# One transpose of 128 columns for the two heads' compressed probabilities, in a decoder layer on one core

## The chip, the cores and the metric

The kernel runs on one core of one Trainium2 chip. The metric is the device time of one execution in microseconds, the median of several runs. The engines are named as in the profile: PE is TensorE (PEld its weight loads), DVE is VectorE, ACT is ScalarE, POOL is GpSimd, and SP issues most of the transfers.

## The reference

One decoder layer over 1024 tokens of width 1024: a joint projection, four heads of differential attention, eight heads of sparse attention in two groups of four (three branches with a gate each: compressed, selected, window), an output projection, and a SwiGLU network, each of the two residual sums under a layer norm. The change is in the compressed branch. Its keys and values are 63 blocks, and every query has a probability for each:

```python
s_c = jnp.einsum('btghd,bngd->btghn', q, kc) * scale
p_cmp = masked_softmax(s_c, mask_c[None, :, None, None, :])
o_cmp = jnp.einsum('btghn,bngd->btghd', p_cmp.astype(dt), vc)
...
o = gates[..., 0:1] * o_cmp + gates[..., 1:2] * o_sel + gates[..., 2:3] * o_win
```

With 1024 tokens all 16 selected blocks are taken, so the selected branch is full causal attention.

## The kernel before

All products are in float32 quality made of float32r operands: a value is split in a high part (a cast on ACT, L81) and a low part (value less high part, a subtraction on DVE, L83, sometimes on POOL), and a product of two such values is three products that add up in one bank (L116, L117, L118). Where one operand has 64 rows, its high and low part share the 128 rows of the array.

The program has stages: the first projections, attention with the rest of the projections as filler, the output projection and first norm, and the network. The attention of the sparse heads is cut into units (nsa_units): a pair p of heads (four pairs), a block i of 128 queries (eight) and a kind, 0 for selected and compressed together, 1 for the window. That makes 32 units of kind 0. A unit has two halves.

The front: score products into the banks psS (L323, L326; two buffers, so a product waits until DVE has read the second last one), on DVE the bias of the distance and the running minimum (L329 for the 64 columns of the compressed blocks, L332 for the rest), on ACT the exponential (L346), then the reciprocal of the sum (L405, DVE) and the scaling by gate and reciprocal (L411, POOL). The compressed probabilities of both heads lie in one tile pc, 128 queries x 2 heads x 64 blocks.

The back: probabilities have to stand with the keys on the rows, so PE transposes them by products with the identity into the banks psT (three buffers, L365), ACT and DVE write high and low part into a tile pt (three buffers; L81 and L83, for pc L371 and L372), and PE multiplies with the values into the bank psO (one buffer). L418 is the first of these products, that of the compressed branch, and opens the sum; L426 and L428 add the high and low parts of the other blocks. The values of the compressed branch (vcc) stand twice, on rows 0 to 63 and again on 64 to 127, with their own high and low part side by side in the columns; thus one product takes the high part of the probabilities on one half of the rows and the low part on the other.

Fronts run two units ahead of backs (look = 2 in the phases). Between them stand filler products of the projections, drawn by a generator (pump, step) in proportion to the work done. The code sets priorities; in which order the instructions of each engine stand in the end is decided by a scheduler, which goes by these priorities and its own idea of durations. Each engine then works through its list in order.

Of the kernel before, what the change touches and what calls it, by code (L numbers as in the profile page):

```python
# [11 lines left out]
F32 = mybir.dt.float32  # L12
# [5 lines left out]
P = 128  # L18
# [7 lines left out]
NC = NCMP + 1  # L26
# [11 lines left out]
def layer_kernel(ctx: ExitStack, tc: tile.TileContext, xT, x, w_t, w_vg, w_dv, lam_in, subln,  # L38
# [4 lines left out]
    nc = tc.nc  # L43
# [10 lines left out]
    def ps_t():  # L54
        return psum.tile([P, 512], F32, tag="T", name="psT", bufs=3)
# [88 lines left out]
    with ExitStack() as ctx_a:  # L144
# [213 lines left out]
            nc.scalar.copy(pt[:, :w], tp[:, :w])  # L358
            return pt

        def transposed(srcs, rows=P):

            tp = ps_t()
            for n, s in enumerate(srcs):
                nc.tensor.transpose(tp[:rows, n * P:(n + 1) * P], s, ident)  # L365
            w = len(srcs) * P
            pt = pt_tile().rearrange("p (h n) -> p h n", h=2)
            if rows == P:
                split(tp[:, :w], pt[:, 0, :w], pt[:, 1, :w])
            else:  # L370
                nc.scalar.copy(pt[0:rows, 0, :w], tp[0:rows, :w])  # L371
                nc.vector.tensor_sub(pt[rows:2 * rows, 0, :w], tp[0:rows, :w], pt[0:rows, 0, :w].bitcast(F32))  # L372
            return pt

        def nsa_units(p, qt, K, V):
# [7 lines left out]
            def make(i, kind):  # L383
                nb = i + 1 if kind == 0 else min(i + 1, WIN_BLOCKS)
                j0 = i + 1 - nb
                width = nb * P
                ts = []

                def front():
                    dist = dsel[:, 1024 - width:] if kind == 0 else dwin[:, 640 - width:]  # L390
                    m = small([P, 4], "m", 4)
                    r = small([P, 4], "r", 4)
                    ts.extend(t_tiles(width))
                    if kind == 0:
                        pc = pa.tile([P, 2, NC], F32, tag="pc", name="pc", bufs=3)
                        ts.append(pc)
                    for a in range(2):
                        ms, rs = ([t[:, n:n + 1] for n in (a, 2 + a)] for t in (m, r))
                        cmp = (pc[:, a, :], dcmp[:, 56 - 8 * i:56 - 8 * i + NC], ms[1]) if kind == 0 else None
                        scores(q_of(qt, i, a), K[kind], j0 * P, width, dist, sl[a], ms[0], ts[a], cmp)  # L400
                        exps(ts[a], width, ms[0], rs[0])
                        if kind == 0:
                            exps(pc[:, a, :], NC, ms[1], rs[1])
                    nr = 2 if kind else 4
                    nc.vector.reciprocal(r[:, :nr], r[:, :nr])  # L405
                    for a in range(2):
                        for n, t in ((1 + kind, ts[a][:, :width]), (0, pc[:, a, :] if kind == 0 else None)):
                            if t is not None:
                                gc = heads[a] * 3 + n
                                c = a if n else 2 + a  # L410
                                nc.gpsimd.tensor_scalar(t, t, r[:, c:c + 1], gates[:, i, gc:gc + 1],  # L411
                                                        op0=ALU.mult, op1=ALU.mult)

                def back(fill):
                    if kind == 0:
                        state["po"] = po = ps_o()
                        ptc = transposed([ts[2][:, a, :] for a in range(2)], rows=64)
                        nc.tensor.matmul(po[:, :256], lhsT=vcc[g], rhs=ptc[:, 0, :256], start=True, stop=False)  # L418
                    po = state["po"]
                    for jj in range(0, nb, 2):  # L420
                        js = range(jj, min(jj + 2, nb))
                        pt = transposed([ts[a][:, j * P:(j + 1) * P] for j in js for a in range(2)])
                        for n, j in enumerate(js):
                            v = V[kind][:, (j0 + j) * P:(j0 + j + 1) * P]
                            last = kind == 1 and j == nb - 1
                            nc.tensor.matmul(po[:, :256], lhsT=v, rhs=pt[:, 0, n * 256:(n + 1) * 256],  # L426
                                             start=False, stop=False)
                            nc.tensor.matmul(po[:, :256], lhsT=v, rhs=pt[:, 1, n * 256:(n + 1) * 256],  # L428
                                             start=False, stop=last)
                        fill((jj + len(js)) / nb)  # L430
                    if kind == 1:
                        tmp = small([P, 256], "tmp", 3)[0:64, :]
                        nc.scalar.copy(tmp, po[64:128, :256])
                        nc.vector.tensor_add(tmp, po[0:64, :256], tmp)
                        for a in range(2):
                            nc.sync.dma_start(mix_d[i, a * 64:(a + 1) * 64, 4 + p, :], tmp[:, a * P:(a + 1) * P])

                return front, back, 2.0 * nb + 1
# [823 lines left out]
```

## Time and profile before

| | |
|---|---|
| time, median of 3 runs | 1308.02 us (1307.05 to 1309.11) |
| span of the profiled execution | 1306.1 us |
| instructions | 20483 |
| granted TensorE clock, mean | 0.999 |
| transposes of pc (L365) | 64, from 98 to 398 us |
| copies L371, subtractions L372, products L418 | 32 each |
| HBM read, written | 116.18 MB, 57.15 MB |

The median is 1.9 us above the span of the profiled execution; the span runs from the first to the last instruction, and no other time of that execution is known. The page gives busy time by engine, a chain of work that ended last, and groups of instructions by line. A line can be that of a helper: L81 and L83 split values for many callers, told apart by their tiles.

### The profile page before, as it was taken

Reading aid. Unit: us, or ns where it says so; the run is one execution under the profiler, and the core shown is the slowest. Engines: PE = TensorE matmul, PEld = TensorE weight load, DVE = VectorE, ACT = ScalarE, POOL = GpSimd, SP = SyncE. Lnnn points to the kernel's source line nnn. Section 1 sums busy time; section 2 is a strip of 40 time slices with the busy share of each in tenths; the row PEclk is TensorE's granted clock in tenths of the full one; section 3 lists DMA queues with packets and bytes.
Section 4 is the critical chain, followed back from the end, with each engine's and each line's share of the span. In section 5 each row is a group of like instructions: output and inputs, shape, how many; then the busy total and the mean of one; then the engine's idle time right before and its main releaser. Section 6 shows DMA issues by size and latency. Waiting matters only on the chain.

```text
span 1306.1 us, 20483 instructions
## 1 busy us (share of the span) xinstructions
PE 1287.4 (99%) x6955; PEld 1108.2 (85%) x6955; DVE 917.0 (70%) x1956; ACT 652.0 (50%) x1398; POOL 465.3 (36%) x499
## 2 busy tenths in 40 slices
PE   9999999999999999999999999999999999999997
PEld 7897999988988889788887888888888888888886
DVE  5548867778778666674787677776767768555588
ACT  5348867878777556652344333333333335533330
POOL 4514534545345446643623313232231222000071
PEclk9999999999999999999999999999999999999999
DMA  9412011211112135623214566555546549768641
GB/s 356 146 27 49 9 50 54 56 48 48 33 56 70 49 82 148 220 93 107 87 69 144 192 225 234 193 172 172 180 150 205 185 172 344 267 199 290 194 169 65
DMA packets 86842, 183.13 MB, mean 140 GB/s; under 512 B 10577, under 2 KB 19153, under 8 KB 86609
## 3 DMA queue, kind: packets, MB, share of 16 engines
q1 hardware_dynamic: 86736, 181.82, 42.8%
q8 instruction: 55, 0.90, 0.3%
q14 instruction: 51, 0.41, 0.1%
HBM read 116.18 MB, written 57.15 MB: 133 GB/s over the span
## 4 chain that ended last, share of the span: by engine, by line
PE 93%; DVE 4%; ACT 1%; issue 1%; DMA 0%; POOL 0%; DVEq 0%; ACTq 0%; POOLq 0%
PE psM L116 11%; PE psM L118 11%; PE psM L117 10%; PE psT L116 6%; PE psT L117 6%; PE psT L118 6%; PE psS L118 6%; PE psS L117 6%; PE psS L116 6%; PE psT L365 4%; PE psS L323 3%; PE psS L326 3%; PE psO L428 2%; PE psO L426 2%; PE psO L481 2%; PE psO L118 2%
## 5 line engine op out<-in xcount | busy, mean ns | idle before, releaser
L346 ACT ACTIVATE t<-t,m 128x384 f32<-128x384 f32 (+7 forms) x192 | 144.2, 752 | 58.8 <-DVE m L332 53.9
L411 POOL TENSOR_SCALAR t<-t,r,gates 128x640 f32<-128x640 f32 (+7 forms) x128 | 100.2, 789 | 186.9 <-DVE r L405 107.8
L116 PE MATMUL psM<-big,w 128*128 128x512 f32 x304 | 120.6, 397 | 0.3 <-DVE slot L171 0.3
L118 PE MATMUL psM<-big,w 128*128 128x512 f32 x304 | 120.1, 396 | 0.0
L117 PE MATMUL psM<-big,w 128*128 128x512 f32 x304 | 119.9, 394 | 0.0
L323 PE MATMUL psS<-slot,q 128*128 128x320 f32 (+10 forms) x304 | 111.5, 369 | 2.9 <-DVE m L332 2.7
L1010 POOL TENSOR_TENSOR half<-half,half 128x512 f32<-128x512 f32 x22 | 33.3, 1515 | 206.6 <-ACT half L1009 206.6
L83 DVE TENSOR_TENSOR pt<-psT,pt 128x512 fp32r<-128x512 f32 (+1 forms) x152 | 91.4, 615 | 13.6 <-ACT pt L81 12.5
L326 PE MATMUL psS<-slot,q 128*128 128x320 f32 (+10 forms) x304 | 99.2, 329 | 0.0
L81 ACT CAST pt<-psT 128x512 fp32r<-128x512 f32 (+1 forms) x152 | 77.6, 526 | 23.3 <-PE psT L365 10.7
L81 ACT CAST big<-slot 128x1024 fp32r<-128x1024 f32 (+1 forms) x54 | 54.4, 1019 | 65.8 <-DVE slot L1002 51.2
L83 DVE TENSOR_TENSOR op<-op 128x1024 fp32r<-128x1024 f32 x44 | 61.3, 1400 | 36.9 <-ACT op L81 36.4
L83 DVE TENSOR_TENSOR big<-slot,big 128x1024 fp32r<-128x1024 f32 (+1 forms) x54 | 63.5, 1181 | 29.5 <-ACT big L81 29.3
L365 PE MATMUL psT<-ident,t 128*128 128x128 f32 x528 | 82.7, 273 | 1.1 <-DVE pt L83 0.9
L81 ACT CAST op<-op 128x1024 fp32r<-128x1024 f32 x44 | 45.9, 1051 | 63.1 <-DMA op<-t_d 60.5
L332 DVE CUSTOM_DVE_ANT_0 t<-psS,dsel 128x384 f32<-128x384 f32 (+9 forms) x128 | 62.4, 493 | 15.0 <-PE psS L326 9.6
L428 PE MATMUL psO<-pt,slot 128*128 128x256 f32 x264 | 72.2, 295 | 0.1
L1014 POOL TENSOR_TENSOR half<-half,half 128x512 f32<-128x512 f32 x22 | 36.5, 1661 | 98.8 <-DVE half L1013 98.6
L426 PE MATMUL psO<-pt,slot 128*128 128x256 f32 x264 | 71.6, 288 | 0.0
L118 PEld LDWEIGHTS psM<-big,w 128*128 128x128 f32 x304 | 57.1, 188 | 11.5
L81 ACT CAST big<-big 128x1024 fp32r<-128x1024 f32 (+1 forms) x49 | 44.2, 912 | 45.3 <-DMA big<-t_d 37.1
L116 PEld LDWEIGHTS psM<-big,w 128*128 128x128 f32 x304 | 57.3, 188 | 10.9 <-DVE slot L171 0.7
(370 smaller groups left out, 3969.0 us busy)
## 6 DMA issues: line engine op xcount, KB each, us to landing
a_d<-slot SPq DMA_DIRECT2D x77, 256.0 KB, 3.1
t_d<-slot SPq DMA_DIRECT2D x77, 256.0 KB, 2.2
q<-q SPq DMA_DIRECT2D x48, 256.0 KB, 2.9
slot<-in_w_up_dram SPq DMA_DIRECT2D x22, 512.0 KB, 3.8
slot<-in_w_down_dram SPq DMA_DIRECT2D x22, 512.0 KB, 3.9
op<-a_d SPq DMA_DIRECT2D x44, 256.0 KB, 3.4
op<-t_d SPq DMA_DIRECT2D x44, 256.0 KB, 4.1
big<-a_d SPq DMA_DIRECT2D x33, 256.0 KB, 3.2
```

The lines of the kernel that those rows point to most:

```text
L81: nc.scalar.copy(hi, src)
L83: eng.tensor_sub(lo, src, hi.bitcast(F32))
L116: nc.tensor.matmul(acc, lhsT=ah, rhs=bh, start=first, stop=False, skip_group_check=more)
L117: nc.tensor.matmul(acc, lhsT=ah, rhs=bl, start=False, stop=False, skip_group_check=more)
L118: nc.tensor.matmul(acc, lhsT=al, rhs=bh, start=False, stop=last, skip_group_check=more)
L323: mm = nc.tensor.matmul(ps[:, :c + part], lhsT=q[0], rhs=k[:, ks], start=True, stop=False)
L326: nc.tensor.matmul(ps[:, :c + part], lhsT=q[1], rhs=k[:, ks], start=False, stop=True)
L346: nc.scalar.activation(t[:, :width], t[:, :width], AF.Exp, bias=m, scale=-1.0, accum_out=r)
L365: nc.tensor.transpose(tp[:rows, n * P:(n + 1) * P], s, ident)
L411: nc.gpsimd.tensor_scalar(t, t, r[:, c:c + 1], gates[:, i, gc:gc + 1], op0=ALU.mult, op1=ALU.mult)
L426: nc.tensor.matmul(po[:, :256], lhsT=v, rhs=pt[:, 0, n * 256:(n + 1) * 256], start=False, stop=False)
L428: nc.tensor.matmul(po[:, :256], lhsT=v, rhs=pt[:, 1, n * 256:(n + 1) * 256], start=False, stop=last)
```

## The change

The two transposes of pc, one for each head with 64 columns, become one of pc as a matrix of 128 columns. The first head's transposed probabilities then come out on rows 0 to 63 of the bank, the second head's on rows 64 to 127, both in the same 128 columns. The copy and the subtraction, which took both heads at once (64 rows x 256 columns), are now made for each head alone (64 rows x 128 columns), so there are two copies and two subtractions. The high part stays on the head's own rows, the low part goes to the other half; the product that uses pt is the same, as the values stand on both halves.

```diff
-        def transposed(srcs, rows=P):
+        def transposed(srcs):
...
-            if rows == P:
-                split(tp[:, :w], pt[:, 0, :w], pt[:, 1, :w])
-            else:
-                nc.scalar.copy(pt[0:rows, 0, :w], tp[0:rows, :w])
-                nc.vector.tensor_sub(pt[rows:2 * rows, 0, :w], tp[0:rows, :w], pt[0:rows, 0, :w].bitcast(F32))
+            split(tp[:, :w], pt[:, 0, :w], pt[:, 1, :w])
+            return pt
+
+        def transposed_cmp(pc):
+
+            tp = ps_t()
+            nc.tensor.transpose(tp[:, :P], pc.rearrange("p a n -> p (a n)"), ident)
+            pt = pt_tile()[:, :2 * P]
+            for a in range(2):
+                own, other = slice(a * NC, (a + 1) * NC), slice((1 - a) * NC, (2 - a) * NC)
+                cs = slice(a * P, (a + 1) * P)
+                nc.scalar.copy(pt[own, cs], tp[own, :P])
+                nc.vector.tensor_sub(pt[other, cs], tp[own, :P], pt[own, cs].bitcast(F32))
             return pt
...
-                        ptc = transposed([ts[2][:, a, :] for a in range(2)], rows=64)
-                        nc.tensor.matmul(po[:, :256], lhsT=vcc[g], rhs=ptc[:, 0, :256], start=True, stop=False)
+                        nc.tensor.matmul(po[:, :256], lhsT=vcc[g], rhs=transposed_cmp(ts[2]), start=True, stop=False)
```

The lines move: the transpose of pc is L374 now, the copies are L379, the subtractions L380, the product of the compressed branch L425 (was L418), the value products L433 and L435 (were L426 and L428); L365, L323 to L346, L81 and L83 keep theirs.

The scheduler puts the instructions of every engine in another order from the first transpose of pc on, until about the end of attention; behind that the order is the same. Two places show how.

The first is PE's list at the first unit of kind 0. Numbers tell buffers apart (psS_1046 and psS_1051 are the two score banks, pt_916 is what L418 uses). Before:

```order
L365 MATMUL psT_913<-ident_74,pc_853 64x128
L365 MATMUL psT_920<-ident_74,t_852 128x128 x3
L365 MATMUL psT_913<-ident_74,pc_853 64x128
L365 MATMUL psT_920<-ident_74,t_852 128x128
L365 MATMUL psT_939<-ident_74,t_852 128x128 x2
L323 MATMUL psS_1046<-slot1_237,q_464 128x128
L326 MATMUL psS_1046<-slot1_237,q_464 128x128
L323 MATMUL psS_1051<-slot1_237,q_465 128x128
L326 MATMUL psS_1051<-slot1_237,q_465 128x128
L418 MATMUL psO_912<-pt_916,vcc0_86 128x256
L426 MATMUL psO_912<-pt_925,slot2_549 128x256
L365 MATMUL psT_966<-ident_74,t_875 128x128 x4
```

Behind these rows come the next score products, L323 into psS_1086. The same place in PE's list now:

```order
L374 MATMUL psT_913<-ident_74,pc_853 128x128
L365 MATMUL psT_921<-ident_74,t_852 128x128 x4
L365 MATMUL psT_940<-ident_74,t_852 128x128 x2
L323 MATMUL psS_1048<-slot1_237,q_464 128x128
L326 MATMUL psS_1048<-slot1_237,q_464 128x128
L323 MATMUL psS_1053<-slot1_237,q_465 128x128
L326 MATMUL psS_1053<-slot1_237,q_465 128x128
L323 MATMUL psS_1088<-slot0_236,q_464 128x288
L326 MATMUL psS_1088<-slot0_236,q_464 128x288
L323 MATMUL psS_1094<-slot0_236,q_464 128x288
L326 MATMUL psS_1094<-slot0_236,q_464 128x288
```

The next score products follow at once, with no product between, and L418, now L425, stands further back, behind six more transposes of t and twelve filler products of 512 columns.

The second place is ACT's list at the second unit, with the engines that an instruction waits for in brackets. Before:

```order
L81 CAST pt<-psT 128x256 [waits DVE_49,PE_49]
L346 ACTIVATE pc,r<-pc,m 128x64 [waits DVE_49,Pool_49]
L371 CAST pt<-psT 64x256 [waits PE_49,Activation_49]
L346 ACTIVATE t,r<-t,m 128x512 [waits DVE_49]
L346 ACTIVATE pc,r<-pc,m 128x64 [waits DVE_49]
```

The one copy waits for the transpose. The same unit in ACT's list now:

```order
L81 CAST pt<-psT 128x256 [waits PE_49]
L379 CAST pt<-psT 64x128 [waits PE_49]
L346 ACTIVATE pc,r<-pc,m 128x64 [waits DVE_49]
L379 CAST pt<-psT 64x128 [waits DVE_49]
L346 ACTIVATE t,r<-t,m 128x512 [waits DVE_49]
```

Of the two copies the first waits for the transpose and the second for DVE: the count that it waits for is reached by the subtraction of the same unit's first head. An exponential stands between them.

More of the change, by code (lines that the diff above doesn't have):

```diff
@@ L359, in transposed_whole @@
             return pt
-        def transposed(srcs, rows=P):
+        def transposed(srcs):
             tp = ps_t()
             for n, s in enumerate(srcs):
-                nc.tensor.transpose(tp[:rows, n * P:(n + 1) * P], s, ident)
+                nc.tensor.transpose(tp[:, n * P:(n + 1) * P], s, ident)
             w = len(srcs) * P
             pt = pt_tile().rearrange("p (h n) -> p h n", h=2)
-            if rows == P:
-                split(tp[:, :w], pt[:, 0, :w], pt[:, 1, :w])
-            else:
-                nc.scalar.copy(pt[0:rows, 0, :w], tp[0:rows, :w])
-                nc.vector.tensor_sub(pt[rows:2 * rows, 0, :w], tp[0:rows, :w], pt[0:rows, 0, :w].bitcast(F32))
+            split(tp[:, :w], pt[:, 0, :w], pt[:, 1, :w])
[9 more added lines that the diff above has]
+                nc.vector.tensor_sub(pt[other, cs], tp[own, :P], pt[own, cs].bitcast(F32))
             return pt
```

## Prediction

> **What bounds the kernel now.** The views were read in this order: the page's busy times and chain, a table of busy time by stretch, the timeline of the matrix engine (PE) around the changed products, the groups of instructions by shape, and the waits of PE in the stretch that holds the change. From the page, the head, the busy times and the chain by engine:
>
> ```profile
> span 1306.1 us, 20483 instructions
> PE 1287.4 (99%) x6955; PEld 1108.2 (85%) x6955; DVE 917.0 (70%) x1956; ACT 652.0 (50%) x1398; POOL 465.3 (36%) x499
> PE 93%; DVE 4%; ACT 1%; issue 1%; DMA 0%; POOL 0%; DVEq 0%; ACTq 0%; POOLq 0%
> ```
>
> PE is the bound: the chain that ended last lies on it for 93%. The rest, 5%, is on the vector (DVE) and scalar (ACT) engines. The changed products stand between 98 and 398 us (first and last start in the row of L365 below), so the stretch from 95 to 408 us is the one to read. The table by stretch gives busy time of PE, PEld, DVE, ACT and POOL, the granted clock and the DMA share:
>
> ```profile
> 95.00:408.00 313.00, 308.74 (x2113) 281.61 (x2112) 239.87 (x845) 239.28 (x645) 145.99 (x212) 1.00 0.18 45
> 408.00:600.00 192.00, 188.32 (x1156) 166.01 (x1156) 129.83 (x364) 111.13 (x292) 99.63 (x98) 1.00 0.39 112
> ```
>
> PE shows 4.3 us idle in 313; DVE is busy for 77% and ACT for 76%, more than in the stretch behind. So a product less on PE should be worth its spacing, and DVE and ACT have room, but not much.
>
> **What a product is worth.** Durations of products overlap, so the price is the distance of starts. The timeline of PE, with start, length and instruction:
>
> ```profile
> 247.37 0.28 PE L426 MATMUL psO<-pt,slot 128*128 128x256 f32 x1
> 247.49 0.38 PE L365 MATMUL psT<-ident,t 128*128 128x128 f32 x2
> 247.63 0.36 PE L428 MATMUL psO<-pt,slot 128*128 128x256 f32 x1
> 247.83 0.27 PE L426 MATMUL psO<-pt,slot 128*128 128x256 f32 x1
> 247.94 0.28 PE L428 MATMUL psO<-pt,slot 128*128 128x256 f32 x1
> 248.06 0.38 PE L365 MATMUL psT<-ident,pc 128*64 128x128 f32 x2
> 248.20 0.45 PE L323 MATMUL psS<-slot,q 128*128 128x448 f32 x1
> 248.48 0.36 PE L326 MATMUL psS<-slot,q 128*128 128x448 f32 x1
> 248.69 0.28 PE L426 MATMUL psO<-pt,slot 128*128 128x256 f32 x1
> 248.80 0.36 PE L323 MATMUL psS<-slot,q 128*128 128x448 f32 x1
> 249.00 0.37 PE L326 MATMUL psS<-slot,q 128*128 128x448 f32 x1
> ```
>
> A 256-wide product takes 0.12 us to the next start (247.83 to 247.94, 247.94 to 248.06) and a 448-wide one 0.20 (248.80 to 249.00). Two transposes of t with the product behind them take 247.83 - 247.49 = 0.34, so 0.22 without it; two of pc take 248.48 - 248.06 = 0.42, less 0.20, again 0.22. A transpose costs 0.11 us, with 64 columns as with 128.
>
> Its weight load, from the groups of line L365 (least, median and longest ns; first and last start):
>
> ```profile
> L365 PEld LDWEIGHTS psT<-ident,t x528: 137/140/147, 98.6 to 404.9; 128*128 128x128 f32 x176
> L365 PEld LDWEIGHTS psT<-ident,pc x64: 108/110/113, 98.4 to 397.6; 128*64 128x64 f32 x64
> ```
>
> The load of 128 columns takes 30 ns more, but two of t take no longer than two of pc, so the work of PE hides it; were it in the open, 32 of them would cost 1.0 us.
>
> **Term 1, the products: 32 fewer at 0.11 us, -3.5 us.** All are on PE, in a stretch where PE sets the pace.
>
> **The copies and subtractions.** The groups by shape (count, busy us, mean ns, idle before them and what ended it): the old forms, then the nearest rows for 64 x 128, and last a pair of groups that alternate as the new ones will.
>
> ```profile
> L371 ACT CAST pt<-psT 64x256 fp32r<-64x256 f32 x32 | 11.5, 361 | 4.2 <-PE psT L365 4.0
> L372 DVE TENSOR_TENSOR pt<-psT,pt 64x256 fp32r<-64x256 f32 x32 | 13.4, 418 | 1.5 <-ACT pt L371 0.7
> L358 ACT COPY pt<-psT 128x128 f32<-128x128 f32 x8 | 2.1, 265 | 0.6 <-PE psO L481 0.5
> L485 DVE COPY od<-psO 128x128 f32<-128x128 f32 x31 | 8.9, 288 | 15.4 <-PE psO L481 15.1
> L83 DVE TENSOR_TENSOR slot<-psT,slot 128x64 fp32r<-128x64 f32 x32 | 6.8, 223 | 11.3 <-ACT slot L81 11.2
> L81 ACT CAST slot<-psT 128x64 fp32r<-128x64 f32 x32 | 6.5, 213 | 11.4 <-PE psT L118 6.1 <-DVE slot L83 5.2
> ```
>
> No 64 x 128 form is in the trace; it lies between 128x64 and 64x256, and 128 columns cost 265 ns on ACT and 288 on DVE. So each unit adds 2 x 265 - 361 = 169 ns on ACT and 2 x 288 - 418 = 158 ns on DVE: 5.4 and 5.1 us in all (ends: with the 128x64 rows 2.1 and 0.9, with the old price twice 11.6 and 13.4). [...]
>
> The second copy also waits. In the order of ACT after the change it stands behind a wait for DVE, that of the unit's first subtraction, so copy, subtraction, copy, subtraction follow one another, four steps in place of two. Queued behind it on ACT are exponentials (L346) and other copies of transposed blocks (L81), for which DVE and then PE wait. The nearest row for it is the last above: there ACT stood 5.2 us for DVE over 32 copies, 0.16 each, so 32 second copies give 5.2 us more idle ACT.
>
> **Term 2, load and waits beside PE: +0.7 us.** That is 15.7 us in all (5.4 + 5.1 + 5.2). DVE and ACT put 5% of 1306, 65 us, on the chain out of 1569 busy, 4.2%; that share of 15.7 is 0.7. The ends are 0 and, if every ACT wait reached PE, 5.2. The cover is the work queued on PE; where it is gone a unit would pay about 0.8 us (a copy of 0.27, a turn of DVE of some 0.5).
>
> **What the new order does to the waits of PE.** The waits of PE and its weight loads in 95 to 408 us (total, times, longest; one wait can be in both views):
>
> ```profile
> PE psS L323 <- DVE m L332: 2.3, 4, 0.9
> PE psO L418 <- DVE pt L372: 0.4, 1, 0.4
> PEld psS L323 <- DVE m L332: 4.1, 9, 1.1
> PEld psO L428 <- DVE pt L83: 2.4, 9, 0.4
> PEld psO L418 <- DVE pt L372: 1.6, 4, 0.6
> ```
>
> I counted the products between a producer and its user in PE's order, at the spacings above. **Term 3, the wait of L418: -0.5 us.** Units with under 2 us of products between the transpose of pc and L418 fall from five to one, and the rows have five waits, 2.0 us; the first is the place that the order shows. But the way to L418 now has four steps. How long turns on two engines take, one unit shows: its pc products are those of 248.06 above.
>
> ```profile
> 249.17 0.37 ACT L371 CAST pt<-psT 64x256 fp32r<-64x256 f32 x1
> 250.97 0.42 DVE L372 TENSOR_TENSOR pt<-psT,pt 64x256 fp32r<-64x256 f32 x1
> 256.30 0.28 PE L418 MATMUL psO<-pt,vcc 128*128 128x256 f32 x1
> ```
>
> The copy began 1.1 us and the subtraction 2.9 us behind the product, and L418 8.2 us behind: here the longer way stays covered by 4.9 us. Ends: all 2.0 us gone, or as much again; I take a quarter of the gain. **Term 4, score products: +1.5 us.** Those that follow the last use of their bank by under 1 us rise from 16 to 22 (the order shows two). Thirteen waits took at most 6.4 us, 0.49 each, so six more cost 0 to 2.9; half is taken, since many are only just under. **Term 5, value products: +0.7 us.** Transposes with under 1.5 us to their first product rise from 7 to 12; at 0.27 a wait (2.4 over 9) 0 to 1.3, half taken. From 408 us on the order changes by places only, up to about 600 us, and not behind that: 0, give or take 1. The edit issues no DMA, and the queues of POOL and SP keep their instructions.
>
> **The sum.** -3.5 + 0.7 - 0.5 + 1.5 + 0.7 = -1.1 us. The profiled span is 1306.1; the median of the three runs, 1308.02 us, holds 1.9 us more around it, which nothing here touches. So 1308.0 - 1.1 = 1306.9 us, a span of 1305.0. The bound for a difference, 0.2%, is 2.6 us; the runs before spread over 2.1.
>
> **The rivals.** *Faster:* terms 2, 4 and 5 are nothing, since the order leaves enough work in front of each user, and L418 waits no more: -3.5 - 2.0 = -5.5, 1302.5 us. For it: PE idles only 4.3 us in the stretch; against: DVE and ACT were already the ones that PE waited for. *Slower:* the second copy blocks ACT until DVE comes to the first subtraction, and L418 and the score products come too early. The price: five units at 0.8 us, 4.0, and the upper ends 2.9 and 1.3, less 3.5: +4.7, 1312.7 us. It decides from 0.11 us of new PE waiting a unit (3.5 / 32) for no gain, and from 0.19 (6.1 / 32) for a loss over 2.6. *The wide product is no cheaper than two:* then term 1 is 0 and the sum +2.4, 1310.4; the equal spacing of pc and t speaks against it. [...]
>
> **How the numbers follow.** The forecast has 0.40 (its own range 1305.4 to 1309.0), faster as above 0.32, slower 0.24, the wide product 0.02, the drain 0.02. Faster by over 0.2% is 0.34, within it 0.42 (the wide product ends there), slower 0.24. The range, 1302.0 to 1312.0 us, takes in the fast rival and most of the slow one, and leaves out the drain and a loss over 4 us.
>
> **What would show it.** Right: L374 32 times, PE's spacing at them 0.11; copies of 64x128 near 265 ns, subtractions near 288; PE's busy time some 3.5 us shorter, with idle and waits for L332 and L83 up by 2 to 3 us. Wrong: waits of L425 (the old L418) over 3 us in total, or ACT standing at L379 for DVE over 8 us (slower); or waits of PE in the stretch no longer than before (faster).

## The result, and the profile after

The kernel after takes 1318.06 us (median of 4 runs, 1316.38 to 1319.8), the kernel before 1307.72 us beside it (1307.05 to 1309.11). The ratio is 1.008, with a 95% interval from 1.0068 to 1.0092: 10.3 us slower, where 1.1 us faster was forecast, and above the stated range, which ended at 1312.0.

From the page of the kernel after, the head, the busy times and the chain by engine:

```profile
span 1314.7 us, 20477 instructions
PE 1289.0 (98%) x6923; PEld 1105.2 (84%) x6923; DVE 923.6 (70%) x1988; ACT 657.1 (50%) x1430; POOL 465.0 (35%) x499
PE 90%; DVE 5%; ACT 2%; issue 2%; DMA 1%; POOL 0%; SPq 0%; DVEq 0%; ACTq 0%; POOLq 0%
```

32 products are gone (6955 to 6923), but PE's busy time has not fallen (1287.4 to 1289.0), where some 3.5 us less was expected, and its part of the chain went from 93% to 90%. The single instructions came out as priced. The groups by shape of the new copies and subtractions (count, busy us, mean ns, idle before them and what ended it):

```profile
L379 ACT CAST pt<-psT 64x128 fp32r<-64x128 f32 x64 | 16.5, 257 | 8.5 <-DVE pt L380 4.0 <-PE psT L374 2.5 <-PE psO L425 1.3
L380 DVE TENSOR_TENSOR pt<-psT,pt 64x128 fp32r<-64x128 f32 x64 | 18.4, 288 | 6.3 <-ACT pt L379 4.4
```

257 and 288 ns a piece, where 265 and 288 were expected, and ACT stands 4.0 us for the subtraction (5.2 expected). The transpose is where it should be too. PE's timeline at one of the 32 (start, length):

```profile
258.75 0.30 PE L326 MATMUL psS<-slot,q 128*128 128x288 f32 x1
258.89 0.27 PE L374 MATMUL psT<-ident,pc 128*128 128x128 f32 x1
258.99 0.39 PE L425 MATMUL psO<-pt,vcc 128*128 128x256 f32 x1
```

0.10 us to the next start. So the prices of single instructions were right, and the time went elsewhere. To find the place I cut the run by two marks that stand in every version: the first transpose of pc, and the first and last transpose of a block of the differential heads (L355). The group of L355 (least, median, longest ns; first and last start), first of before, then of after:

```profile
L355 PE MATMUL psT<-ident,t x144: 270/272/328, 405.5 to 596.0; 128*128 128x128 f32 x144
```

```profile
L355 PE MATMUL psT<-ident,t x144: 270/273/332, 411.0 to 604.6; 128*128 128x128 f32 x144
```

The last one comes 8.6 us later, and the span is longer by 8.6 (1306.1 to 1314.7): all of the loss between these two executions lies in front of 604.6 us. The profiled execution of the kernel after took 1316.38 us at a mean granted clock of 0.999 and the other three 1317.69 to 1319.8 at 0.998 and 0.997, so the traces show 8.6 us of the 10.3 between the medians. The loss is in two stretches. The table by stretch (length, then busy time of PE, PEld, DVE, ACT, POOL, the clock and the DMA share), of before and of after:

```profile
98.60:405.50 306.90, 302.63 (x2075) 276.17 (x2074) 236.26 (x828) 234.69 (x628) 142.17 (x203) 1.00 0.18 46
405.50:596.00 190.50, 186.82 (x1159) 165.21 (x1158) 130.63 (x368) 112.17 (x294) 99.02 (x99) 1.00 0.39 112
```

```profile
98.50:411.00 312.50, 303.84 (x2043) 273.10 (x2042) 241.99 (x860) 240.55 (x660) 141.39 (x203) 1.00 0.18 45
411.00:604.60 193.60, 187.38 (x1159) 165.55 (x1158) 130.60 (x368) 111.77 (x294) 99.54 (x99) 1.00 0.37 110
```

In the stretch with the changed units, 5.6 us more (306.9 to 312.5), with 32 products fewer and PE's idle time doubled, from 4.3 to 8.7 us. In the stretch behind it, 3.1 us more (190.5 to 193.6), and there the products are the same 1159: the edit changes no work in it, only the order. The waits of PE and of its weight loads between 95 and 411 us (total, times, longest):

```profile
PE psT L365 <- DVE pt L83: 3.0, 6, 1.3
PE psS L323 <- DVE m L332: 2.3, 4, 0.8
PE psS L323 <- issue: 1.1, 1, 1.1
PE psS L323 <- DVE m L329: 0.3, 1, 0.3
PE psT L365 <- DVE pt L380: 0.3, 1, 0.3
PE psO L425 <- DVE pt L380: 0.2, 1, 0.2
```

```profile
PEld psS L323 <- DVE m L332: 6.1, 15, 0.9
PEld psT L365 <- issue: 3.6, 7, 1.7
PEld psO L435 <- DVE pt L83: 3.3, 12, 0.4
PEld psS L323 <- issue: 2.3, 5, 1.3
```

The same rows of the kernel before, where they were not shown yet (95 to 410 us):

```profile
PE psT L365 <- DVE pt L83: 0.9, 2, 0.7
```

```profile
PEld psT L365 <- issue: 1.3, 5, 0.4
...
PEld psS L323 <- issue: 0.5, 2, 0.3
```

The product that uses the new copies, L425, hardly waits (0.2). The waits that grew belong to other work: the transposes of t, which stand until DVE has freed a bank (0.9 before, 3.0 now), the weight loads of score products (4.1 to 6.1), and weight loads for whose wait the trace names no releaser ("issue", 1.8 to 5.9). That pointed at the order of the lists, not at the changed instructions.

### The profile page after: what moved, and what is told of

It is laid out like the page before. It is cut to its first block, busy times and chain, and to the rows that moved or that the text cites. A ratio compares the mean times of both kernels' runs of the same rounds, so it can differ in the third digit from the quotient of the medians.

```text
span 1314.7 us, 20477 instructions
## 1 busy us (share of the span) xinstructions
PE 1289.0 (98%) x6923; PEld 1105.2 (84%) x6923; DVE 923.6 (70%) x1988; ACT 657.1 (50%) x1430; POOL 465.0 (35%) x499
## 4 chain that ended last, share of the span: by engine, by line
PE 90%; DVE 5%; ACT 2%; issue 2%; DMA 1%; POOL 0%; SPq 0%; DVEq 0%; ACTq 0%; POOLq 0%
PE psM L116 10%; PE psM L118 10%; PE psM L117 10%; PE psT L116 6%; PE psT L117 6%; PE psT L118 6%; PE psS L118 6%; PE psS L116 6%; PE psS L117 6%; PE psT L365 4%; PE psS L323 3%; PE psS L326 3%; PE psO L435 2%; PE psO L433 2%; PE psO L116 2%; PE psO L118 2%
## 5 line engine op out<-in xcount | busy, mean ns | idle before, releaser
L346 ACT ACTIVATE t<-t,m 128x384 f32<-128x384 f32 (+7 forms) x192 | 144.0, 751 | 55.0 <-DVE m L332 51.3
L323 PE MATMUL psS<-slot,q 128*128 128x320 f32 (+10 forms) x304 | 111.4, 370 | 7.8 <-DVE m L332 4.0
L83 DVE TENSOR_TENSOR pt<-psT,pt 128x512 fp32r<-128x512 f32 (+1 forms) x152 | 91.7, 614 | 11.3 <-ACT pt L81 10.5
L83 DVE TENSOR_TENSOR op<-op 128x1024 fp32r<-128x1024 f32 x44 | 60.6, 1386 | 41.4 <-ACT op L81 41.1
L81 ACT CAST pt<-psT 128x512 fp32r<-128x512 f32 (+1 forms) x152 | 77.5, 527 | 24.1 <-PE psT L365 13.5
L81 ACT CAST big<-slot 128x1024 fp32r<-128x1024 f32 (+1 forms) x54 | 54.4, 1018 | 68.4 <-DVE slot L1009 54.8
L365 PE MATMUL psT<-ident,t 128*128 128x128 f32 x528 | 81.8, 273 | 3.6 <-DVE pt L83 3.0
L83 DVE TENSOR_TENSOR big<-slot,big 128x1024 fp32r<-128x1024 f32 (+1 forms) x54 | 63.8, 1188 | 28.4 <-ACT big L81 28.4
L81 ACT CAST op<-op 128x1024 fp32r<-128x1024 f32 x44 | 45.9, 1051 | 66.7 <-DMA op<-t_d 61.2
L323 PEld LDWEIGHTS psS<-slot,q 128*128 128x128 f32 x304 | 57.4, 189 | 17.0 <-DVE m L332 9.0
L435 PE MATMUL psO<-pt,slot 128*128 128x256 f32 x264 | 71.3, 292 | 0.2
L433 PE MATMUL psO<-pt,slot 128*128 128x256 f32 x264 | 70.8, 287 | 0.0
L365 PEld LDWEIGHTS psT<-ident,t 128*128 128x128 f32 x528 | 61.6, 140 | 9.2 <-issue 3.6
L116 PEld LDWEIGHTS psM<-big,w 128*128 128x128 f32 x304 | 57.2, 188 | 12.4 <-ACT w L81 1.6
```

Source lines behind the costliest of these rows:

```text
L81: nc.scalar.copy(hi, src)
L83: eng.tensor_sub(lo, src, hi.bitcast(F32))
L116: nc.tensor.matmul(acc, lhsT=ah, rhs=bh, start=first, stop=False, skip_group_check=more)
L323: mm = nc.tensor.matmul(ps[:, :c + part], lhsT=q[0], rhs=k[:, ks], start=True, stop=False)
L346: nc.scalar.activation(t[:, :width], t[:, :width], AF.Exp, bias=m, scale=-1.0, accum_out=r)
L365: nc.tensor.transpose(tp[:, n * P:(n + 1) * P], s, ident)
```

## The experiments

The theory at this point (A): the loss belongs to the order that the scheduler made, and the edit's own work gains about what was forecast. Its rival (B): the serial copy, subtraction, copy, subtraction of each unit is the loss. To tell them apart, work and order have to be set apart. A table with each engine's list is put in and kept by chaining every instruction to the one ahead of it in the table:

```diff
+    pin(tc)
...
+    for engine, places in zip(engines, lists):
+        mine = [i for i in traced if i.engine == engine and "PoolBoundary" not in type(i).__name__]
+        for a, b in zip(places, places[1:]):
+            tc.add_manual_dep(mine[b], mine[a].name, how, reason="pinned order")
```

"In the order of" means this below, and "free" that the scheduler decides. All experiments together, each against the kernel before in the same comparison (1307.5 to 1307.8 us). "Wide product alone" leaves out the second head's compressed probabilities, so it is a measure of time only. Two rows whose intervals overlap are not told apart by these runs:

| run | work | order | us | ratio, 95% interval |
|---|---|---|---|---|
| e1 | old | of after | 1318.62 | 1.0086 (1.0072 to 1.0099) |
| e9 | wide product alone | of after | 1316.35 | 1.0071 (1.0059 to 1.0084) |
| e5 | new, copies first | of after | 1345.58 | 1.0286 (1.0272 to 1.0300) |
| e2 | new | of before | 1333.12 | 1.0193 (1.0179 to 1.0207) |
| e3 | new, copies first | of before | 1316.09 | 1.0066 (1.0052 to 1.0079) |
| e8 | as e3, pc scaled early | of before | 1310.19 | 1.0022 (1.0013 to 1.0031) |
| e6 | split alone | of before | 1322.99 | 1.0119 (1.0105 to 1.0132) |
| e7 | split alone, copies first | of before | 1308.79 | 1.0010 (1.0002 to 1.0019) |
| e10 | old | free, another | 1308.07 | 1.0001 (0.9992 to 1.0009) |
| e11 | split alone, copies first | free | 1308.83 | 1.0006 (0.9998 to 1.0015) |
| e15 | split alone | free | 1324.70 | 1.0130 (1.0116 to 1.0143) |
| e14 | wide product alone | free | 1311.47 | 1.0031 (1.0019 to 1.0042) |
| e4 | new, copies first | free | 1315.07 | 1.0057 (1.0044 to 1.0069) |
| e12 | new, pc scaled first | free | 1312.30 | 1.0036 (1.0023 to 1.0049) |
| e16 | new, both of these | free | 1312.67 | 1.0039 (1.0025 to 1.0052) |
| e13 | old | of after behind 405 us only | 1313.20 | 1.0039 (1.0026 to 1.0051) |
| e17 | new | of before behind 411 us only | 1316.06 | 1.0063 (1.0049 to 1.0077) |
| e18 | as e16 | of before behind 406 us only | 1314.38 | 1.0048 (1.0035 to 1.0060) |

### The order apart from the work: e1, e9

> The work of the kernel before (64 transposes of 64 columns, 32 copies and 32 subtractions of 64x256), with every engine's list fixed in the order of the kernel after: the two transposes stand where the one of 128 columns stands, the copy where the first copy stands, the subtraction where the second one stands. Theory A, the order: the loss of 10.3 us is the order's, and the edit's own work gains about as much as forecast (3.5 less 0.7), so this takes the loss and pays the products again: 1318 + 3 = about 1321 us (1318 to 1324). Theory B, the work: the serial copy, subtraction, copy, subtraction of each unit delays PE, and the order does nothing: about 1308 us (1306 to 1310). Between, half each: about 1313.

Measured 1318.62, 11.2 us over before. Its groups of L365 and L355:

```profile
L365 PE MATMUL psT<-ident,pc x64: 270/272/276, 97.9 to 402.9; 128*64 128x128 f32 x64
L355 PE MATMUL psT<-ident,t x144: 270/272/328, 411.0 to 606.7; 128*128 128x128 f32 x144
```

All 64 narrow transposes are there, nothing of the edit's work is, and the marks at 411.0 and 606.7 are late as in the kernel after. Rival B falls: the order alone loses as much as the whole change. But of A's 3 us of gain in this order, only 1318.62 - 1318.06 = 0.6 is there, less than the intervals can tell from nothing. The wide product by itself tells more:

```diff
-            for a in range(2):
-                ...
-                nc.scalar.copy(pt[own, cs], tp[own, :P])
-                nc.vector.tensor_sub(pt[other, cs], tp[own, :P], pt[own, cs].bitcast(F32))
+            both = tp[0:NC, None, :P].to_broadcast([NC, 2, P])
+            nc.scalar.copy(hi, both)
+            nc.vector.tensor_sub(lo, both, hi.bitcast(F32))
```

> The wide product alone: one transpose of 128 columns in place of two of 64, but one copy and one subtraction of 64x256 as before, every list in the order of the kernel after (the run of the old work in that order, with two narrow transposes at this place, took 1318.6 us). The copy and the subtraction read the first head's rows twice, so the second head's compressed probabilities are replaced by the first's; nothing else is changed. If a transpose less is worth its spacing of 0.11 us where PE is the bound: 1318.6 - 3.5 = 1315.1 (1314.3 to 1316). If the wide product is no cheaper, or what it frees is lost in waits at once: 1318 to 1319.

1316.35, just above the range that its spacing gave (1314.3 to 1316): 32 transposes fewer are worth 2.3 us here by the medians. In the two traces the stretch from the first transpose of pc to the first L355 is 1.8 us shorter (313.1 in e1, 311.3 in e9). That is half to two thirds of the 3.5. The split with its chain then costs 1318.06 - 1316.35 = 1.7. Neither 2.3 nor 1.7 is clear of the intervals; only the first step of the account, 11.2 for the order, is. The three steps go from the kernel before to the kernel after, so that their sum, 11.2 - 2.3 + 1.7 = 10.6, comes near the 10.3 by construction and proves nothing further.

### The new work in the old order: e2, e3, e8

The transpose takes the place of the second narrow one (in nine units a place nearer to the first). In e3 the copies are written first:

```diff
-            for a in range(2):
-                ...
-                nc.scalar.copy(pt[own, cs], tp[own, :P])
-                nc.vector.tensor_sub(pt[other, cs], tp[own, :P], pt[own, cs].bitcast(F32))
+            for own, other, cs in halves:
+                nc.scalar.copy(pt[own, cs], tp[own, :P])
+            for own, other, cs in halves:
+                nc.vector.tensor_sub(pt[other, cs], tp[own, :P], pt[own, cs].bitcast(F32))
```

> The work of the kernel after (32 transposes of 128 columns, 64 copies and 64 subtractions of 64x128, the second copy still waiting for the first subtraction), with every engine's list fixed in the order of the kernel before: the transpose stands where the second narrow one stood (in nine units a little earlier, next to the first), the two copies where the copy stood, the two subtractions where the subtraction stood. Theory A, the order: 1308 - 3.5 + 0.7 = about 1305 us (1303 to 1308). Theory B, the work: about 1318 us (1315 to 1321).

> As the run before (new work, old order), but both copies are written ahead of both subtractions, so that the second copy no longer waits for DVE. Theory A, the order: the wait is hidden anyway, so the same as with the wait, within 1.5 us: about 1305 us. Theory B, the work in a serial chain: the wait is the cost, so about 1306 where the run with the wait takes 1318.

1333.12 and 1316.09. Theory A as it stood falls here: it wanted 1305 for both. B misses both times as well (1318 and 1306), though it has the sign of the difference. The old order is no home for the new work, and in it the wait that A held to be hidden costs 17.0 us. Part of e3's loss is the place: four transposes stood for GpSimd's scaling of the second head (PE in e3, 95 to 410 us):

```profile
PE psT L374 <- POOL pc L419: 4.6, 4, 1.5
```

> The new work with copies first in the old order, as run once at 1316.1 us; there four transposes of pc stood 4.6 us for GpSimd's scaling of the second head, since they stand where the first narrow transpose stood. Here, in the nine units with such a place, the scaling of pc's second head is moved ahead of the scaling of t's second head, which gives the transpose 0.9 to 1.1 us. If those waits are an effect of the place only, and the gain of the products is real: 1310 to 1313. If the old order cannot take the wide transpose at all: 1315 to 1317.

The edit is one of the table: the scaling of pc's second head moves one place up in GpSimd's list, at eight places (the tables of e3 and e8 differ in eight pairs of neighbours there and nowhere else). 1310.19, as the place alone would have it (1310 to 1313), and the row above is down to 0.3. That is 5.9 us for four waits and what hung on them, and it is the best time that the whole new work reached; still 2.7 over before.

### The copies and subtractions alone: e6, e7, e11, e15

```diff
-                nc.scalar.copy(pt[0:rows, 0, :w], tp[0:rows, :w])
-                nc.vector.tensor_sub(pt[rows:2 * rows, 0, :w], tp[0:rows, :w], pt[0:rows, 0, :w].bitcast(F32))
+                for n in range(2):
+                    cs = slice(n * P, (n + 1) * P)
+                    nc.scalar.copy(pt[0:rows, 0, cs], tp[0:rows, cs])
+                    nc.vector.tensor_sub(pt[rows:2 * rows, 0, cs], tp[0:rows, cs], pt[0:rows, 0, cs].bitcast(F32))
```

The narrow transposes stay. In e7 and e11 the loop over n is made twice, copies first.

> The kernel before in its own order, the two narrow transposes kept, but with the copy and the subtraction of each unit made as two of 64x128, the second copy waiting for the first subtraction; the copies stand next to each other, and so do the subtractions. This is the split alone, without the wide product and without a new order. By the forecast's term for it: 1308.2 (0.7 more). If the chain costs as much as the earlier pair of runs in the old order differed by (1333.1 with the wait, 1316.1 without): 1318 to 1325.

> As the run before (the split alone, old order, narrow transposes), with both copies ahead of both subtractions, so without the second copy's wait. What is left is 5 us more of busy time on ACT and on DVE each. If only the wait costs: 1307.5 to 1308.5. If busy time costs PE by its whole amount: 1312 to 1313.

1322.99 and 1308.79: 14.2 us for the wait, 1.3 (0.3 to 2.5 by its interval) for 32 instructions more on each engine. The forecast's 1308.2 for e6 is out, and the range taken from e2 and e3 holds; e7 is 0.3 above its range for the wait alone. The groups of the copies, first with the wait, then without:

```profile
L373 ACT CAST pt<-psT 64x128 fp32r<-64x128 f32 x64 | 16.4, 257 | 34.1 <-DVE pt L374 30.4 <-PE psT L365 3.5
```

```profile
L373 ACT CAST pt<-psT 64x128 fp32r<-64x128 f32 x64 | 13.2, 256 | 4.2 <-PE psT L365 4.0
```

With the two copies next to each other in ACT's list, the second stands 30.4 us for DVE, 0.95 each, and everything behind it on ACT stands with it. In one unit of e6 the first copy ends at 202.84 us, DVE comes to the subtraction at 203.44, behind a subtraction of 0.69 us for another block (L83), and the second copy starts at 203.76. The same two with the scheduler free:

> Narrow transposes, the copy and the subtraction split in two each, copies first, with the scheduler free. The same work in the order of the kernel before took 1308.8 us, so the difference to that is the new order's alone (1877 of PE's places changed). If orders that the scheduler makes differ by up to 10 us on their own: 1303 to 1319, off from 1308.8 by over 2. If only the order of the kernel after is a bad one by chance of its chain: 1307 to 1311.

> Two narrow products, copy and subtraction split in two each with the second copy waiting for the first subtraction, the scheduler free (2633 of PE's places changed). With copies first, so without that wait, the free order took 1308.8 us. If the chain leads the scheduler to costly orders: 1313 to 1322. If the wide product does: 1308 to 1311.

1308.83 and 1324.70. Without the wait another order (1877 places of PE changed) takes what the old order takes, to 0.04 us. With the wait the free order costs 15.9 us more (1313 to 1322 was expected if the chain leads to costly orders), though ACT's wait is nearly gone from it (e15):

```profile
L373 ACT CAST pt<-psT 64x128 fp32r<-64x128 f32 x64 | 16.3, 255 | 8.0 <-DVE pt L374 3.1 <-PE psT L365 3.0 <-PE psO L420 1.4
```

The scheduler moved the second copy away from the first until it seldom waited; the time did not come back with the wait. The kernel after has the same row with 4.0 us. How far its lists are built around that chain, e5 shows.

> The kernel after in its own order on every engine, but with both copies written ahead of both subtractions, so that the second copy no longer waits for the first subtraction (every copy and subtraction keeps its place in its list). The old work in this order took 1318.6 us and the new work 1318.1. Theory A, the order sets the time and the chain of copy, subtraction, copy, subtraction hides the gain of the products in it: the rest of the 3.5 us comes out, about 1315 to 1316. Theory A2, the order alone, with the chain hidden: 1318, no change. Theory B, the chain is the whole loss: about 1308.

1345.58, a miss for all three. With copies first, it is the first subtraction that waits for the second copy, and in this order the second copy stands some rows further back in ACT's list (in one unit the first copy starts at 252.70, two copies of L81 follow, and the second starts at 253.94). DVE's wait, 95 to 420 us:

```profile
DVE pt L380 <- ACT pt L378: 36.8, 27, 3.7
```

So this run does not price the chain; it shows that an order fits one sequence of the four steps and not the other.

### Other orders and the two parts, free: e10, e4, e12, e14, e16

e10 writes the narrow transposes in the other sequence; e12 scales pc first, and e16 is that with copies first:

```diff
-            for n, s in enumerate(srcs):
+            for n, s in list(enumerate(srcs))[::-1 if rows < P else 1]:
```

```diff
-                        for n, t in ((1 + kind, ts[a][:, :width]), (0, pc[:, a, :] if kind == 0 else None)):
+                        for n, t in ((0, pc[:, a, :] if kind == 0 else None), (1 + kind, ts[a][:, :width])):
```

> The kernel before with the two narrow transposes written in the other sequence, second head first. The work is the same to the last instruction; the scheduler draws another order, with 597 of PE's places changed between the first pc transpose and about 300 us (the change under study alters 2586, up to the end of attention). If a new order by itself moves the time by us: anywhere from 1303 to 1314, off from 1307.5 by over 1.5. If the order does nothing unless work is added: 1306.5 to 1308.5.

> The kernel after with both copies written ahead of both subtractions, so that the second copy no longer waits for DVE; the scheduler is free again and makes a third order. Theory A, the order: the time is that of a new order, which this theory can't tell beforehand; 1304 to 1322, with PE's waits in the stretches 95 to 410 and 410 to 620 us changed in both. Theory B, the serial chain: about 1306 us (1304 to 1309), the stretch behind 410 us as in the kernel before.

> The kernel after with GpSimd's scaling of each head's pc written ahead of that of its t; no work is added or removed, and the scheduler draws another order. If the loss of 10.3 us is the luck of one order: a time that lies elsewhere, 1305 to 1320, off from 1318.1 by over 2. If it belongs to the work (any order that has the serial copy, subtraction, copy, subtraction): 1317 to 1319.

> The wide product alone (one copy and one subtraction of 64x256 as before, reading the first head's rows twice, so the second head's compressed probabilities are replaced by the first's), the scheduler free. If the wide product, which needs both heads' scaled probabilities at one place, is what leads the scheduler to costly orders: 1311 to 1318. If the serial chain of copies and subtractions is: 1304 to 1306, the products' gain.

> The whole new work, both copies ahead of both subtractions, and GpSimd's scaling of each head's pc written ahead of that of its t; the scheduler is free. Each of the two alone took 1315.1 and 1312.3 us, the kernel after 1318.1. If they are independent faults: about 1309. If every such order is a draw of its own: 1304 to 1318. Only under 1306 would it beat the kernel before.

A new order need not cost anything (e10: 1308.07 with 597 of PE's places changed, e11: 1308.83 with 1877). With the new work, free orders differ by up to 5.8 us (1318.06, 1315.07, 1312.30, 1312.67), so the loss of 10.3 is partly that of one order. But none of them comes near 1307.5 (theory B's 1304 to 1309 for e4 is out, and A's 1304 to 1322 could hardly fail), and the two mends are not independent (1312.67 with both, 1309 wanted). In these orders the chain costs far less than in e6 and e15: 3.0 us between the kernel after and e4, and nothing between e12 and e16 (1312.30 with it, 1312.67 without). e14 has neither split nor chain and is 3.8 us over before, so the wide product has a part of its own in it:

```profile
L355 PE MATMUL psT<-ident,t x144: 270/273/417, 404.6 to 602.5; 128*128 128x128 f32 x144
```

Up to the first L355 it is 0.9 us ahead of the kernel before (404.6 against 405.5), of the 3.5 that its products should bring; then it loses 7.4 (602.5 - 404.6 = 197.9, against 190.5). The profiled execution of e14 took 1314.61 us, 3.1 more than the median, and up to 1.7 us of the 7.4 (an estimate, half of the 3.4 us that follow) are not the order's but the clock's. From 561.8 us on, the granted clock is 0.50 for 3.4 us. PE behind a wait of 1.8 us, and the clock (the sixth figure behind the length) from 562 to 563 us:

```profile
561.30 0.50 PE L116 MATMUL psM<-big,w 128*128 128x512 f32 x1 [1.82 <-ACT w L81]
561.90 0.63 PE L116 MATMUL psM<-big,w 128*128 128x512 f32 x1
562.32 0.63 PE L117 MATMUL psM<-big,w 128*128 128x512 f32 x1
```

```profile
562.00:563.00 1.00, 1.00 (x5) 0.70 (x4) 1.00 (x4) 1.00 (x5) 0.00 (x0) 0.50 0.00 0
```

The starts are 0.42 us apart in place of 0.23 (566.77 to 567.00 in the same trace). Other traces have such slices of 3.4 us as well, each at a wait of PE or within some 3 us behind one: e1, e4, e8 and e17 one each, e15 two, e5 five. That of e1 starts at 514.6 us, behind 2.2 us of waiting, so up to 1.7 us of its 11.2 may be the clock's, too. The kernels before and after have none in the stretches read here, and neither has e13, where PE stands 3.0 us. That the waits bring the slices on is suggested by their places; no run tests it. If they do, a wait of PE can cost up to 1.7 us (an estimate, half of 3.4) beyond itself.

### The stretch that the edit doesn't touch: e13, e17, e18

> The old work, every list in the old order up to the first block of the differential heads (L355, 405 us) and in the order of the kernel after from there on. The whole new order cost 11 us with the old work. If the order behind 405 us loses by itself, as the stretch from the first to the last L355 says (190.5 us before, 195.7 with the new order): 1312 to 1313. If that stretch is late only because of what came before it: 1307 to 1308.5.

1313.20: the order of the kernel after costs 5.5 us from 405 us on alone, with the old work all through. The profiled execution took 1311.58; in it the stretch from the first to the last L355 takes 194.5 us, 4.0 more than before. One place holds 3.0 us of waiting. In e13 (DVE, SP's queue, then PE; behind PE's row its wait):

```profile
499.88 0.74 DVE L177 SCALAR_TENSOR_TENSOR q<-psM,qscale,q 128x512 fp32r<-128x512 f32 x1
500.65 5.69 SPq L161 DMA_DIRECT2D q<-q  x3
508.93 0.30 PE L323 MATMUL psS<-slot,q 128*128 128x128 f32 x1 [2.99 <-DMA q<-q]
```

The same three in the kernel before:

```profile
497.60 0.75 DVE L177 SCALAR_TENSOR_TENSOR q<-psM,qscale,q 128x512 fp32r<-128x512 f32 x1 [0.22 <-ACT q L176]
498.38 4.83 SPq L161 DMA_DIRECT2D q<-q  x3
505.94 0.31 PE L323 MATMUL psS<-slot,q 128*128 128x128 f32 x1
```

Before, the product starts 7.6 us behind the first of the transfers that bring its queries, and needn't wait. In the new order PE comes to it at the same time, 508.93 - 2.99 = 505.94, but the transfers leave 2.3 us later, since DVE comes later to the instruction that writes the queries (L177, 499.88 against 497.60). PE is there 5.3 us behind them and stands for 3.0. In the kernel after it is this product, too, that waits longest in this stretch, though the trace names another releaser:

```profile
513.49 0.30 PE L323 MATMUL psS<-slot,q 128*128 128x128 f32 x1 [1.79 <-DVE od L492]
```

> The kernel after, in its own order up to the first block of the differential heads (L355, 411 us) and in the order of the kernel before from there on. Its stretch from the first to the last L355 took 193.5 us, 190.5 in the kernel before. If the order behind 405 us loses by itself: 1318.1 - 3 to 4.5, 1313.6 to 1315.1, with the rest of the loss, 5 to 7 us, in the compressed units. If that stretch only hands on a delay: 1317 to 1319.

> The whole new work with both copies first and pc scaled first (1312.7 us with the scheduler free), its own order up to the first block of the differential heads, and the order of the kernel before from there on. If the stretch behind loses by its order alone, 194.9 - 190.5 = 4.4 us come off: 1308.3 (1307 to 1310), which is the time of the kernel before; the products' 3.5 us are then used up by waits and by the added work. To beat the kernel before by what can be measured it would need less than 1305.

1316.06 and 1314.38: the old order behind the new work gives back 2.0 us in one case and takes 1.7 in the other, where 3 to 4.5 were expected of both. Neither is clear of the intervals (the kernel after 1.0068 to 1.0092, e16 1.0025 to 1.0052), and both expectations miss. The groups of L355, of e17 and of e18:

```profile
L355 PE MATMUL psT<-ident,t x144: 270/272/329, 411.4 to 604.4; 128*128 128x128 f32 x144
```

```profile
L355 PE MATMUL psT<-ident,t x144: 270/272/328, 406.3 to 601.5; 128*128 128x128 f32 x144
```

193.0 and 195.2 us, with the lists that took 190.5 behind the old work. Two waits are in them that the kernel before lacks or has shorter, for the queries again and for weights (PE, e18, 405 to 615 us):

```profile
PE psS L323 <- DMA q<-q: 1.1, 1, 1.1
PE psM L116 <- ACT w L81: 1.0, 1, 1.0
```

They hold 2.1 of the 4.7 us. Other runs with the old lists point the same way, each by one trace: the stretch takes 190.7 and 190.2 us in e6 and e7, with narrow transposes, and 191.5 to 192.7 in e2, e3 and e8, with the whole new work. Why the same list runs slower behind the new work is not settled. No version beat the kernel before.

## Why the prediction was wrong, point by point

**What bounds the kernel: right.** PE is it, with 93% of the chain before and 90% after.

**Term 1, -3.5: price right, worth less.** A transpose takes its 0.10 to 0.11 us. Where the rest of the order stays, the 32 are worth 2.3 by the medians and 1.8 by the traces (e9 against e1). PE's busy time was to fall by 3.5 and rose by 1.6: between the first transpose of pc and the first L355 the order alone adds 3.2 (302.63 before, 305.85 in e1).

**Instruction prices: right** (257 and 288 ns); ACT's busy time grew by 5.1 us, DVE's by 6.6, of which 5.0 are the subtractions (13.4 to 18.4).

**Term 2, +0.7, ends 0 and 5.2: mis-sized, and its upper end was no bound.** The load alone is 1.3 (e7). The wait, taken at 0.16 us from the evacuation of the values, is 0.95 where the lists are not built around it (e6), because DVE here has work of its own in front of the subtraction. And its price to PE was 14.2 us for 30.4 us of ACT's waiting there, not the 4% that the page's chain gave: a share averaged over the run was no price for an engine held up in the middle of its list. In the order of the kernel after, product and split together come to -0.6 (-2.3 + 1.7), where terms 1 and 2 said -2.8.

**Term 3, -0.5: right in sign.** L425 waits 0.2 us on PE, where L418 waited 0.4 there and 1.6 at its weight loads.

**Terms 4 and 5, +1.5 and +0.7: right as far as they went.** The weight loads of score products wait 2.0 us more (4.1 to 6.1), those of the value products 0.9 more (2.4 to 3.3). What had no term is the transposes of t that stand for a bank (2.1 more) and the rows of both L323 and L365 in which the trace names no releaser (5.9 us of weight loads against 1.8).

**The step that failed** is the price of the new order. Terms 3 to 5 put it at -0.5 + 1.5 + 0.7 = 1.7 us, and one line put the rest at nothing: "From 408 us on the order changes by places only, up to about 600 us, and not behind that: 0, give or take 1." With not one instruction of the edit the order costs 11.2 us (e1). The larger part of the miss is in the stretch with the changed units, which takes 5.6 us more where 1.1 less was forecast: terms 3 to 5 count places at three users that were chosen beforehand, and the waits that grew are in part those of others. The smaller part is the stretch behind, 3.1 us more in the kernel after, and by its order alone, with the old work, 4.0 in the trace and 5.5 by the medians (e13).

**The rivals.** "Slower" had the right side and not the mechanism: neither five units with L425 too early nor ACT blocked for over 8 us (4.0). So neither sign of "slower" came, and the kernel was slower still. The wide product "no cheaper" has e9 against it, if not clear of the intervals. The drain, which has 0.02 in the chances, was a supposition that a narrow product costs PE more than its spacing; no run shows it: 32 wide products in place of 32 pairs of narrow ones gave 2.3 us (e9 against e1), less than the 3.5 of their spacing. That a chain of four steps would lead the scheduler to another order, and that this could be the cost, was not among them.

**Shown:** the order carries the loss (e1), the chain costs 14 to 17 us in the old order (e2 and e3, e6 and e7), and with narrow transposes even a free order is 15.9 us worse with it (e11 and e15). **Argued only:** that the order of the kernel after is costly because the scheduler, too, worked around the chain. Against it speaks that, with the wide product and free orders, leaving the chain out gave 3.0 us (e4, whose interval just touches that of the kernel after) or nothing (e12 and e16); the wide product without the chain also led to costly orders (e14, e4, e16), for a reason that stays open.

## What to carry to other kernels

Where a scheduler rewrites every list, put the old work into the new order before explaining anything by the work: that one run held the whole loss (11.2 us, e1), and it also shows that a stretch that the edit does not touch is not worth zero. Two engines that took turns on the halves of one bank did better with all steps of the first engine ahead of the second's: in the old order the split itself was 1.3 us, the turn-taking 14. A list made for the one sequence does not fit the other, though (e5, 1345.58 us). Counting places at a few users bounds those users, not the order.

## What the runs showed that I had not expected

Two microseconds between a transfer and its user decided whether a score product stood for its queries: the one that came 7.6 us behind the first of three transfers found them there, the one that came 5.3 behind stood until 8.3. A wait of PE of 1.8 us was followed by 3.4 us at a granted clock of 0.50 in e14, and one of 3.0 us in e13 was not. And a list that is fixed to the last instruction, with the same work in it, took 190.5, 193.0 or 195.2 us, depending on what ran ahead of it, each in one execution; the granted clock is 1.00 in that stretch in all three.
